# Silu at the ends of convolution blocks, k and q weighting behind the substitution, three casts on VectorE, in a two-layer hybrid encoder

## The chip, the cores and the metric

The kernel runs on one core of a Trainium2 chip. A core has the engines PE (TensorE), DVE (VectorE), ACT (ScalarE), POOL (GpSimd) and SP (SyncE, which only issues transfers here), each working through its own instructions in order, and 16 DMA engines that serve all queues. The metric is the device time of one execution in microseconds (us). For each kernel several executions are timed and the median counts.

## The reference, cut to what matters

Two layers over 256 rows of width 1024, fp32 throughout. Each layer has one wide input projection, a gated delta branch (8 heads of 128, a short convolution over q, k and v), a differential attention branch (8 heads), and a gated merge with an output projection.

```python
qkv = jax.nn.silu(short_conv(jnp.concatenate([q, k, v], axis=-1), conv_w))
q, k, v = jnp.split(qkv, (GDN_QK, 2 * GDN_QK), axis=-1)
q = l2norm(heads(q, GDN_DK)); k = l2norm(heads(k, GDN_DK)); v = heads(v, GDN_DV)
g = -jnp.exp(a_log) * jax.nn.softplus(ab[2:] + dt_bias)
...
L = jnp.where(strict, jnp.einsum('bhncd,bhnmd->bhncm', kb, k) * decay, 0.0)
T = lax.linalg.triangular_solve(eye + L, eye, lower=True, unit_diagonal=True)
...
qk = jnp.where(lower, jnp.einsum('bhncd,bhnmd->bhncm', q, k) * decay, 0.0)
S_t = a_t (I - b_t k_t k_t^T) S_(t-1) + b_t k_t v_t^T;  o_t = S_t^T q_t   (both directions)
y_a = rmsnorm(o) * silu(z_a);   y_b = attention(q_b, k_b, v_b) * silu(z_b)
x = x + (sigmoid(gate_a) * (y_a @ w_pa) + sigmoid(gate_b) * (y_b @ w_pb)) @ w_out
```

## The kernel before

**Projections.** A weight block of 1024 x 512 is loaded in four parts (kp 0 to 3, 512 KB each, by SP's queue) into three buffers called raw. Each part is split in two fp32r halves: ACT casts raw to hi (L230), DVE subtracts to get lo (L232). PE multiplies the activations hT with hi, again with the other half, and with lo (L244 to L246 row-major, accumulators pp_; L298 to L302 feature-major, accumulators pf_). hi and lo have two buffers each, so a part is cast when PE has finished with the part two before it. Projections are named by what they make: k, q, v of the delta branch (two blocks g of four each), qk (four: q and k of the attention branch), vb, zb, za, gb, pb, ga, pa, o.

**Convolution.** conv() runs a feature-major projection and closes each of its four 128-channel blocks: ACT writes the middle tap (cvq and the like, L523), four DVE instructions add the other taps (L527), ACT takes tanh of half the sum (thq, L531), and DVE multiplies (th + 1) * conv (L536), which is twice the Silu; the factor is taken out in the norms. Eight blocks each of k, q and v make 24 a layer. The result lies in kq; PE turns it (ctk, ctq, L544) and ACT sums its squares (sqj).

**Decays.** log_decays() takes the logarithms of gates and norms on ACT (Ln, L572), turns them into running sums with PE (grps) and copies those to grow on DVE (L588). POOL writes them to DRAM (gdr, L591) and decays() reads each of four groups back, spread to all partitions (B, 512 KB each, L618). POOL masks them (L624) and ACT takes 8 exps of 128x128 a group (L628). weigh_k() takes the grams of k (kk, PE, L611) and multiplies them with the summed decays into A (L635). weigh_q() multiplies the grams of q and k (kq) into B (L639).

**Substitution.** A goes through DRAM (adr) to la and lt; 31 steps on DVE (L670, L671) solve the triangular systems in X. spread_blocks() copies X to lt (L674), POOL writes both to DRAM (udr, L678), and blocks T and U are read back. merges() and chunks() then run the chunked recurrence on PE (zt, qs, ks and the like), with ktm, the turned k, weighted by POOL (L795). The attention heads (sc, mx, es: scores, maximum, exps; L839 to L848) and the zb and za projections run beside the substitution.

**What sets the order.** The program is written in the order of its calls, and a scheduler places each engine's instructions by priority; the loads and splits of weights run under high priority, ahead of their place. tc.issue_after(ins) keeps an instruction behind another one (held in the dictionary mark). SP's and POOL's queues take their transfers in that order too, and an instruction that waits holds up all behind it on its engine.

## Time and profile before

| | us |
|---|---|
| median of 3 runs | 779.93 |
| lowest, highest | 778.48, 781.05 |
| span of the profiled execution | 777.1 |
| PE busy | 758.2 |
| DVE busy | 557.3 |
| ACT busy | 474.9 |
| POOL busy | 101.9 |

The profiled execution has no time of its own beside its span; the runs lie 1.4 to 4.0 above that span. Busy time says how long an engine worked; with several engines, only the waits of the one that sets the end are worth something. The granted clock of PE is 1.00 in all windows but the last.

### The profile page before, as it was taken

How to read it: one execution, taken by the hardware profiler on the slowest of the kernel's cores; microseconds unless marked ns; L12 is line 12 of the kernel's file. 1: busy time of each engine (PE TensorE's matmuls, PEld its weight loads, DVE VectorE, ACT ScalarE, POOL GpSimd, SP SyncE). 2: the span in 40 equal slices, each digit the busy share in tenths (PEclk: the TensorE clock that was granted, in tenths of full speed). 3: DMA queues.
4: the chain of work that ended last, by engine and by line, in shares of the span. 5: the costliest groups of instructions: out<-in, count | busy, mean ns of one | idle time of the engine just before them, and what ended most of it. 6: DMA issues, size and time to landing. Idle time of an engine off the chain costs nothing.

```text
span 777.1 us, 13805 instructions
## 1 busy us (share of the span) xinstructions
PE 758.2 (98%) x5222; PEld 647.7 (83%) x5222; DVE 557.3 (72%) x1051; ACT 474.9 (61%) x1042; POOL 101.9 (13%) x137
## 2 busy tenths in 40 slices
PE   8999999999999999999999999999999999999996
PEld 4899879887778888887889888899777788888784
DVE  5686878999974635377677776989999553536782
ACT  5657776557677744564554668655577776356551
POOL 5100461100030100010010025510001110001000
PEclk9999999999999999999999999999999999999998
DMA  7752756554496644346664256755446954343631
GB/s 227 240 177 78 224 146 198 174 172 136 112 207 187 210 135 129 117 144 210 215 224 136 82 160 221 194 170 161 141 137 174 233 164 160 114 133 111 213 110 54
DMA packets 77745, 126.91 MB, mean 163 GB/s; under 512 B 19679, under 2 KB 20015, under 8 KB 77680
## 3 DMA queue, kind: packets, MB, share of 16 engines
q1 hardware_dynamic: 71038, 112.99, 48.4%
q0 software_dynamic: 3936, 9.77, 4.8%
q10 hardware_dynamic: 2706, 3.28, 1.3%
q8 instruction: 41, 0.67, 0.4%
q14 instruction: 24, 0.20, 0.1%
HBM read 121.27 MB, written 4.75 MB: 162 GB/s over the span
## 4 chain that ended last, share of the span: by engine, by line
PE 81%; DVE 7%; DMA 5%; ACT 4%; issue 2%; POOL 0%; SPq 0%; POOLq 0%; ACTq 0%; DVEq 0%
PE pp_vb L282 5%; DMA raw_q<-in_w_in_dram 3%; PE pp_qk L245 2%; PE pp_qk L246 2%; PE pp_qk L244 2%; PE pp_o L282 2%; PE pf_k L298 2%; PE pf_k L302 2%; PE pf_v L298 2%; PE pf_k L300 2%; PE pp_gb L245 2%; PE sc L839 2%; PE pp_gb L244 2%; PE pf_v L302 2%; PE pf_v L300 2%; PE av L865 2%
## 5 line engine op out<-in xcount | busy, mean ns | idle before, releaser
L245 PE MATMUL pp_qk<-lo_qk,hT 128*128 128x512 f32 x128 | 51.3, 401 | 1.0 <-DVE lo_qk L232 1.0
L246 PE MATMUL pp_qk<-hi_qk,hT 128*128 128x512 f32 x128 | 50.1, 391 | 0.0
L230 ACT CAST hi_qk<-raw_qk 128x1024 fp32r<-128x1024 f32 x32 | 33.5, 1046 | 23.6 <-PE pp_qk L246 12.6
L244 PE MATMUL pp_qk<-hi_qk,hT 128*128 128x512 f32 x128 | 46.1, 398 | 0.7 <-ACT hi_qk L230 0.7
L232 DVE TENSOR_TENSOR lo_qk<-raw_qk,hi_qk 128x1024 fp32r<-128x1024 f32 x32 | 40.2, 1257 | 7.6 <-ACT hi_qk L230 7.4
L232 DVE TENSOR_TENSOR lo_pb<-raw_pb,hi_pb 128x1024 fp32r<-128x1024 f32 x16 | 19.6, 1224 | 35.7 <-ACT hi_pb L230 35.7
L298 PE MATMUL pf_q<-hT,hi_q 128*128 128x256 f32 x128 | 36.5, 288 | 0.3 <-ACT hi_q L230 0.2
L298 PE MATMUL pf_v<-hT,hi_v 128*128 128x256 f32 x128 | 36.5, 289 | 0.0
L300 PE MATMUL pf_v<-hT,hi_v 128*128 128x256 f32 x128 | 36.2, 286 | 0.0
L300 PE MATMUL pf_q<-hT,hi_q 128*128 128x256 f32 x128 | 35.9, 284 | 0.0
L848 ACT ACTIVATE es<-sc,mx 128x256 f32<-128x256 f32 x64 | 29.8, 473 | 10.1 <-DVE mx L846 10.0
L298 PE MATMUL pf_k<-hT,hi_k 128*128 128x256 f32 x128 | 35.8, 285 | 0.0
L302 PE MATMUL pf_q<-hT,lo_q 128*128 128x256 f32 x128 | 35.7, 292 | 0.0
L300 PE MATMUL pf_k<-hT,hi_k 128*128 128x256 f32 x128 | 35.7, 283 | 0.0
L232 DVE TENSOR_TENSOR lo_gb<-raw_gb,hi_gb 128x1024 fp32r<-128x1024 f32 x16 | 19.6, 1224 | 22.2 <-ACT hi_gb L230 22.0
L232 DVE TENSOR_TENSOR lo_ga<-raw_ga,hi_ga 128x1024 fp32r<-128x1024 f32 x16 | 19.6, 1226 | 21.0 <-ACT hi_ga L230 21.0
L302 PE MATMUL pf_v<-hT,lo_v 128*128 128x256 f32 x128 | 34.6, 286 | 0.0
L302 PE MATMUL pf_k<-hT,lo_k 128*128 128x256 f32 x128 | 34.4, 285 | 0.0
L230 ACT CAST hi_pb<-raw_pb 128x1024 fp32r<-128x1024 f32 x16 | 16.8, 1049 | 25.1 <-PE pp_pb L246 24.3
L527 DVE SCALAR_TENSOR_TENSOR cvq<-pf_q,cw,cvq 128x254 f32<-128x254 f32 (+1 forms) x64 | 29.7, 476 | 1.8 <-ACT cvq L523 1.4
L527 DVE SCALAR_TENSOR_TENSOR cvv<-pf_v,cw,cvv 128x254 f32<-128x254 f32 (+1 forms) x64 | 30.2, 483 | 0.6 <-ACT cvv L523 0.5
L527 DVE SCALAR_TENSOR_TENSOR cvk<-pf_k,cw,cvk 128x254 f32<-128x254 f32 (+1 forms) x64 | 28.5, 478 | 2.0 <-ACT cvk L523 1.3
(356 smaller groups left out, 2495.5 us busy)
## 6 DMA issues: line engine op xcount, KB each, us to landing
raw_qk<-in_w_in_dram SPq DMA_DIRECT2D x32, 512.0 KB, 3.7
raw_k<-in_w_in_dram SPq DMA_DIRECT2D x16, 512.0 KB, 4.6
raw_q<-in_w_in_dram SPq DMA_DIRECT2D x16, 512.0 KB, 3.7
raw_v<-in_w_in_dram SPq DMA_DIRECT2D x16, 512.0 KB, 3.8
raw_zb<-in_w_in_dram SPq DMA_DIRECT2D x16, 512.0 KB, 3.6
raw_za<-in_w_in_dram SPq DMA_DIRECT2D x16, 512.0 KB, 3.7
raw_gb<-in_w_in_dram SPq DMA_DIRECT2D x16, 512.0 KB, 4.7
raw_o<-in_w_out_dram SPq DMA_DIRECT2D x16, 512.0 KB, 4.5
```

The lines of the kernel that those rows point to most:

```text
L230: high = S.copy(hi[:, :, :n], raw[:, :, :n]).ins
L232: mark[nm, kp] = high, V.tensor_tensor(lo[:, :, :n], raw[:, :, :n], hi[:, :, :n].bitcast(F32), ALU.subtract).ins
L244: T.matmul(o, act[kt // 4][:, 0, kt % 4, ts_], hi, start=kt == 0, stop=False)
L245: T.matmul(o, act[kt // 4][:, 0, kt % 4, ts_], lo, start=False, stop=False)
L246: mark["proj"] = T.matmul(o, act[kt // 4][:, 1, kt % 4, ts_], hi, start=False, stop=kt == KT - 1).ins
L282: mark["proj"] = T.matmul(o, a_, w_, start=kt == 0 and a_ is ah and w_ is hi, stop=kt == KT - 1 and a_ is al).ins
L298: T.matmul(o, hi[:, cs], act[kt // 4][:, 0, kt % 4, :], start=first, stop=False, skip_group_check=True)
L300: T.matmul(o, hi[:, cs], act[kt // 4][:, 1, kt % 4, :], start=False, stop=False, skip_group_check=True)
L302: T.matmul(o, lo[:, cs], act[kt // 4][:, 0, kt % 4, :], start=False, stop=done, skip_group_check=True)
L527: V.scalar_tensor_tensor(ca[:, o0:o1], acc[:, b, o0 + sft : o1 + sft], cw[:, j, cb : cb + 1], ca[:, o0:o1], ALU.mult, ALU.add)
L839: mm = T.matmul(sp[n][:, qt * SEQ : (qt + 1) * SEQ], qkT[h // 4][rows, 0, h % 4, qt * P : (qt + 1) * P], qkT[h // 4][rows, 1, h % 4, :], s ...
L848: S.activation(es[:, n, qt, :], spv[:, qt, :], AF.Exp, bias=mx[:, n, qt : qt + 1], accum_out=s_all[:, h, n, qt : qt + 1])
```

## The change

- **Silu.** In 18 of 24 convolution blocks a layer ACT writes Silu of the sum straight into kq (or into the buffer vf for v). The six blocks in HALF (the first four of q and the last two of v) keep tanh and the product, with taps scaled by 0.5 once a layer. Since the result is no longer doubled, the constants in the norms change.
- **Weighting.** weigh_q() moves from beside the q convolutions to behind the fifth head, and its kq grams are held behind marks of the merges. The k weighting stays in its call order, and ktm's product on POOL is held behind a udr write.
- **Casts.** Three weight parts a layer (the last of q's second block, the first two of the second qk block) are cast by DVE (turned).
- **Broadcasts.** The third and fourth decays() pass the last exps of the first group to issue_after for their transfer.

```diff
--- before.py
+++ after.py
@@ -26,6 +26,7 @@
 EPS = 1e-6
+HALF = (0, 1, 2, 3, 22, 23)
 HP = None
@@ -204,7 +205,7 @@
-    def weights(w, c0, n, nm, homes=(None,) * 4, ahead=True, later=None, spare=(), held=None):
+    def weights(w, c0, n, nm, homes=(None,) * 4, ahead=True, later=None, spare=(), held=None, turned=()):
@@ -227,17 +228,17 @@
                 with behind(act):
-                    high = S.copy(hi[:, :, :n], raw[:, :, :n]).ins
+                    high = (V.tensor_copy if kp in turned else S.copy)(hi[:, :, :n], raw[:, :, :n]).ins
                 with behind(dve):
...
-    def proj_tm(act, w, c0, n, evac, nm, places=(None,) * 4, spare=(), later=None):
+    def proj_tm(act, w, c0, n, evac, nm, places=(None,) * 4, spare=(), later=None, turned=()):
         accs = banks2(f"pp_{nm}")
-        for kt, hi, lo in weights(w, c0, n, nm, places, later=later, spare=spare):
+        for kt, hi, lo in weights(w, c0, n, nm, places, later=later, spare=spare, turned=turned):
             for m in range(NM):
@@ -284,11 +285,11 @@
-    def proj_fm(act, w, c0, evac, nm):
+    def proj_fm(act, w, c0, evac, nm, turned=()):
...
         accs = [a.rearrange("p (b t) -> p b t", b=2) for a in banks2(f"pf_{nm}")]
-        for kt, hi, lo in weights(w, c0, 512, nm, later=mark.pop("later", None)):
+        for kt, hi, lo in weights(w, c0, 512, nm, later=mark.pop("later", None), turned=turned):
             for b in range(4):
@@ -415,6 +416,8 @@
         V.tensor_copy(cw.rearrange("p t b -> p (t b)"), cw_ps[:, : TAPS * 24])
+        for b0, b1 in ((0, 4), (22, 24)):
+            V.tensor_scalar(cw[:, :, b0:b1], cw[:, :, b0:b1], 0.5, None, ALU.mult)
         prm = small.tile([P, 2, 16], F32, tag="prm", name=f"prm{l}")
@@ -455,7 +458,8 @@
                           pt.rearrange("p (b t) -> p b t", b=4), (DH ** -0.5, 1.0)[s_])
-                proj_tm(hT, wl, (C_QB, C_KB)[s_] + 512 * i, 512, evac_qk, f"qk{l}{s_}{i}")
+                proj_tm(hT, wl, (C_QB, C_KB)[s_] + 512 * i, 512, evac_qk, f"qk{l}{s_}{i}",
+                        turned=(0, 1) if (s_, i) == (0, 1) else ())
@@ -524,18 +528,19 @@
                         o0, o1 = max(0, -sft), SEQ - max(0, sft)
-                        V.scalar_tensor_tensor(ca[:, o0:o1], acc[:, b, o0 + sft : o1 + sft],
-                                               cw[:, j, cb : cb + 1], ca[:, o0:o1],
-                                               ALU.mult, ALU.add)
-                    th = work.tile([P, SEQ], F32, tag="vf", name=f"th{seg}{l}{g}{j4}", bufs=2)
-                    S.activation(th, ca, AF.Tanh, scale=0.5)
-                    if slot is None:
-                        f_ = th.rearrange("p (m t) -> p m t", m=NM)
+                        mark["conv"] = V.scalar_tensor_tensor(
+                            ca[:, o0:o1], acc[:, b, o0 + sft : o1 + sft],
+                            cw[:, j, cb : cb + 1], ca[:, o0:o1], ALU.mult, ALU.add).ins
+                    cm = ca.rearrange("p (m t) -> p m t", m=NM)
+                    if slot is None or cb in HALF:
+                        th = work.tile([P, SEQ], F32, tag="vf", name=f"th{seg}{l}{g}{j4}", bufs=2)
+                        tm = th.rearrange("p (m t) -> p m t", m=NM)
+                    f_ = tm if slot is None else kq[:, 4 * g + j4, :, slot, :]
+                    if cb in HALF:
+                        S.activation(tm, cm, AF.Tanh)
+                        V.scalar_tensor_tensor(f_, tm, 1.0, cm, ALU.add, ALU.mult)
                     else:
-                        f_ = kq[:, 4 * g + j4, :, slot, :]
-                    mark["conv"] = V.scalar_tensor_tensor(
-                        f_, th.rearrange("p (m t) -> p m t", m=NM), 1.0,
-                        ca.rearrange("p (m t) -> p m t", m=NM), ALU.add, ALU.mult).ins
+                        S.activation(f_, cm, AF.Silu)
                     vf.append(f_)
@@ -555,7 +560,8 @@
                                      accum_out=ss[:, m, hd : hd + 1])
-            proj_fm(hT, wl, c_base + 512 * g, evac_conv, f"{seg}{l}{g}")
+            proj_fm(hT, wl, c_base + 512 * g, evac_conv, f"{seg}{l}{g}",
+                    turned=(3,) if (seg, g) == ("q", 1) else ())
@@ -564,9 +570,9 @@
             kss = e_[:, :, 32:40]
-            V.tensor_scalar(kss, ssk, 4.0 * EPS, None, ALU.add)
+            V.tensor_scalar(kss, ssk, EPS, None, ALU.add)
             kh = small.tile([P, NM, NH], F32, tag="kh", name=f"kh{l}")
-            V.tensor_scalar(kh, kss, 1.0 / 16.0, None, ALU.mult)
+            V.tensor_scalar(kh, ssk, EPS, None, ALU.add)
             G.tensor_tensor(nrm.rearrange("p m h -> p (m h)"), kh.rearrange("p m h -> p (m h)"),
@@ -604,19 +610,21 @@
-        def gram(nm, g, c, slot):
+        def gram(nm, g, c, slot, after=None):
             gp = bank_c(f"{nm}{l}{g}{c}")
...
                 kqh = kq[:, 4 * g + j4, c]
-                T.matmul(gp[:, j4 * P : (j4 + 1) * P], kqh[:, 0, :], kqh[:, slot, :],
-                         start=True, stop=True)
+                with behind(after):
+                    T.matmul(gp[:, j4 * P : (j4 + 1) * P], kqh[:, 0, :], kqh[:, slot, :],
+                             start=True, stop=True)
             return heads4(gp)
-        def decays(g, c):
+        def decays(g, c, after=None):
             hs4 = slice(4 * g, 4 * g + 4)
             dec = B[:, c, hs4].rearrange("p h d i -> p d h i")
-            G.dma_start(out=B[:, c, hs4].rearrange("p h d i -> p (h d i)"),
-                        in_=gdr[c, hs4].rearrange("h d i -> (h d i)").partition_broadcast(P))
+            with behind(after):
+                G.dma_start(out=B[:, c, hs4].rearrange("p h d i -> p (h d i)"),
+                            in_=gdr[c, hs4].rearrange("h d i -> (h d i)").partition_broadcast(P))
             end = (P - 1) * (1 - c)
@@ -625,8 +633,8 @@
                     h = 4 * g + j4
-                    S.activation(dec[:, d, j4, :], dec[:, d, j4, :], AF.Exp,
-                                 bias=lnc[:, d, c, h : h + 1])
+                    mark["decay", d] = S.activation(dec[:, d, j4, :], dec[:, d, j4, :], AF.Exp,
+                                                    bias=lnc[:, d, c, h : h + 1]).ins
@@ -634,9 +642,9 @@
-        def weigh_q(g, c):
+        def weigh_q(g, c, after):
             bv = B[:, c, 4 * g : 4 * g + 4]
-            V.tensor_tensor(bv, gram("kq", g, c, 1).unsqueeze(2).to_broadcast([P, 4, 2, P]), bv, ALU.mult)
+            V.tensor_tensor(bv, gram("kq", g, c, 1, after).unsqueeze(2).to_broadcast([P, 4, 2, P]), bv, ALU.mult)
@@ -671,12 +679,12 @@
         def spread_blocks():
-            V.tensor_copy(lt, X.rearrange("p c i -> p i c"))
+            mark["spread"] = V.tensor_copy(lt, X.rearrange("p c i -> p i c")).ins
             for d in range(2):
...
                 for w, src_ in enumerate((X, lt) if d == 0 else (lt, X)):
-                    G.dma_start(out=udr[w, :, :, 8 * d : 8 * d + 8].rearrange("b g t j i -> (b g) (t j i)"),
-                                in_=src_[ps_].rearrange("p j i -> p (j i)"))
+                    mark["udr"] = G.dma_start(out=udr[w, :, :, 8 * d : 8 * d + 8].rearrange("b g t j i -> (b g) (t j i)"),
+                                in_=src_[ps_].rearrange("p j i -> p (j i)")).ins
@@ -792,7 +800,8 @@
             for d in range(2):
-                G.tensor_tensor(st[d], st[d], last(kds[:, d, hs4], P), ALU.mult)
+                with behind(mark["udr"]):
+                    G.tensor_tensor(st[d], st[d], last(kds[:, d, hs4], P), ALU.mult)
                 ps = four(f"sp{d}", lambda j: st[d][:, j, :], lambda j: y1[d][:, j, :])
@@ -896,20 +905,17 @@
         weigh_k(0, 0)
+        seen = mark["decay", 0], mark["decay", 1]
         decays(0, 1)
         weigh_k(0, 1)
-        decays(1, 0)
+        decays(1, 0, seen[0])
         weigh_k(1, 0)
-        decays(1, 1)
+        decays(1, 1, seen[1])
         weigh_k(1, 1)
         turn_blocks()
-        weigh_q(0, 0)
-        weigh_q(0, 1)
         conv("q", C_QA, 1, 1)
...
         qk_part(0, 1)
-        weigh_q(1, 0)
-        weigh_q(1, 1)
         substitute(0, 31)
@@ -928,6 +934,9 @@
         head(5)
+        for g in range(2):
+            for c in range(NM):
+                weigh_q(g, c, mark["done", 4 * g + 2 * c + 1])
         z_part(za, C_ZA, "za", 1)
@@ -982,7 +991,7 @@
         rq = small.tile([P, NM, NH], F32, tag="rq", name=f"rq{l}")
-        V.tensor_scalar(rq2, ssq, 0.25 * P, EPS * P, ALU.mult, ALU.add)
+        V.tensor_scalar(rq2, ssq, float(P), EPS * P, ALU.mult, ALU.add)
         G.tensor_tensor(rq.rearrange("p c h -> p (c h)"), rq2.rearrange("p c h -> p (c h)"),
```

Where instructions stand now. First ACT around the second q convolution block in layer 0: hi_q are weight casts of that block (its first one stands three rows ahead of this piece), stg copies of the first qk projection, B the exps of the decays, thq and cvq the first q block. Before:

```order
L443 COPY stg_1059<-pp_qk_985 128x512
L230 CAST hi_q_1234<-raw_q_1236 128x1024
L443 COPY stg_1072<-pp_qk_986 128x512
L531 ACTIVATE thq_964<-cvq_958 128x256
L523 ACTIVATE cvq_967<-pf_q_810,cw_268 128x256
L556 ACTIVATE sqj_280,ssq_333<-ctq_949 128x128 x2
L230 CAST hi_q_1264<-raw_q_1266 128x1024
L556 ACTIVATE sqj_280,ssq_333<-ctq_949 128x128
L456 ACTIVATE qkT_0_281<-qkt_1066 128x4x128
L556 ACTIVATE sqj_280,ssq_333<-ctq_949 128x128
L628 ACTIVATE B_340<-B_340,lnc_336 128x128 x8
L230 CAST hi_q_1294<-raw_q_1296 128x1024
```

After (L numbers of the changed program), from the second row behind the first hi_q on:

```order
L540 ACTIVATE thq_932<-cvq_926 128x256
L636 ACTIVATE B_342<-B_342,lnc_338 128x128 x4
L446 COPY stg_1045<-pp_qk_971 128x512
L636 ACTIVATE B_342<-B_342,lnc_338 128x128 x4
L540 ACTIVATE thq_950<-cvq_944 128x256
L231 CAST hi_q_1208<-raw_q_1210 128x1024
L446 COPY stg_1058<-pp_qk_972 128x512
L527 ACTIVATE cvq_953<-pf_q_796,cw_268 128x256
L636 ACTIVATE B_342<-B_342,lnc_338 128x128 x7
L561 ACTIVATE sqj_282,ssq_335<-ctq_935 128x128
L636 ACTIVATE B_342<-B_342,lnc_338 128x128
L231 CAST hi_q_1238<-raw_q_1240 128x1024
```

Eight exps now stand ahead of the block's second cast and eight more ahead of its third, where before the third stood ahead of all of them. 

DVE around grow in the same layer: lo_qk are the low halves of the first qk block, cvq taps of the first q block, ge, lnc, glog the gate logarithms. Before:

```order
L232 TENSOR_TENSOR lo_qk_1006<-raw_qk_1007,hi_qk_1005 128x1024
L573 SCALAR_TENSOR_TENSOR ge_315<-ga_312,ge_315 128x2x32
L527 SCALAR_TENSOR_TENSOR cvq_931<-pf_q_809,cw_268,cvq_931 128x254
L576 SCALAR_TENSOR_TENSOR lnc_336<-ge_315 128x16 x2
L579 TENSOR_TENSOR glog_788<-ge_315,nega_273 128x32
L232 TENSOR_TENSOR lo_qk_1024<-raw_qk_1025,hi_qk_1023 128x1024
L536 SCALAR_TENSOR_TENSOR kq_329<-thq_937,cvq_931 128x2x128
L527 SCALAR_TENSOR_TENSOR cvq_940<-pf_q_809,cw_268,cvq_940 128x254
L527 SCALAR_TENSOR_TENSOR cvq_940<-pf_q_809,cw_268,cvq_940 128x255
L588 COPY grow_795<-grps_790 8x512
L527 SCALAR_TENSOR_TENSOR cvq_940<-pf_q_809,cw_268,cvq_940 128x255
L232 TENSOR_TENSOR lo_qk_1042<-raw_qk_1043,hi_qk_1041 128x1024
```

After:

```order
L233 TENSOR_TENSOR lo_q_888<-raw_q_889,hi_q_887 128x1024
L579 SCALAR_TENSOR_TENSOR ge_317<-ga_314,ge_317 128x2x32
L582 SCALAR_TENSOR_TENSOR lnc_338<-ge_317 128x16 x2
L585 TENSOR_TENSOR glog_774<-ge_317,nega_275 128x32
L233 TENSOR_TENSOR lo_qk_974<-raw_qk_975,hi_qk_973 128x1024
L531 SCALAR_TENSOR_TENSOR cvq_917<-pf_q_795,cw_268,cvq_917 128x254
L531 SCALAR_TENSOR_TENSOR cvq_917<-pf_q_795,cw_268,cvq_917 128x255
L594 COPY grow_781<-grps_776 8x512
L531 SCALAR_TENSOR_TENSOR cvq_917<-pf_q_795,cw_268,cvq_917 128x255
L233 TENSOR_TENSOR lo_qk_992<-raw_qk_993,hi_qk_991 128x1024
```

The gate logarithms now stand ahead of the first lo_qk, and grow behind that and two taps of the first q sub-block.

POOL from the k weighting to the writes of the substitution's result. Before:

```order
L795 TENSOR_TENSOR ktm_330<-ktm_330,kds_341 128x512 x4
L654 DMA adr_342<-A_339 32x16x32 x4
L656 DMA la_344<-adr_342 64x1024
L657 DMA lt_345<-adr_342 64x1024
L658 MEMSET X_346 128x1024
L659 MEMSET X_346 128x32
L986 TENSOR_TENSOR rq_3662<-rq_3661,mhalf 128x16
L678 DMA udr_343<-X_346 8x8x1024 x2
L678 DMA udr_343<-lt_345 8x8x1024 x2
```

After:

```order
L662 DMA adr_344<-A_341 32x16x32 x4
L664 DMA la_346<-adr_344 64x1024
L665 DMA lt_347<-adr_344 64x1024
L666 MEMSET X_348 128x1024
L995 TENSOR_TENSOR rq_3634<-rq_3633,mhalf 128x16
L667 MEMSET X_348 128x32
L686 DMA udr_345<-X_348 8x8x1024 x2
L804 TENSOR_TENSOR ktm_332<-ktm_332,kds_343 128x512 x4
L686 DMA udr_345<-lt_347 8x8x1024 x2
```

The four ktm products moved from ahead of the adr writes to between the two pairs of udr writes. On SP's queue, the four loads of U now stand ahead of the last raw_za load; before, they stood behind it, one raw_gb load and four loads of T.

## The prediction

> **What bounds the kernel now.** I read the page's busy row and chain first, then the windows, then PE's waits.
>
> ```profile
> span 777.1 us, 13805 instructions
> PE 758.2 (98%) x5222; PEld 647.7 (83%) x5222; DVE 557.3 (72%) x1051; ACT 474.9 (61%) x1042; POOL 101.9 (13%) x137
> PE 81%; DVE 7%; DMA 5%; ACT 4%; issue 2%; POOL 0%; SPq 0%; POOLq 0%; ACTq 0%; DVEq 0%
> ```
>
> PE works in 98% of the span, and the change leaves PE's matmuls as they are. A faster kernel can only come from the 777.1 - 758.2 = 18.9 us in which PE stands. The windows (span, then PE busy and its instructions, then PEld, DVE, ACT, POOL) say where they lie:
>
> ```profile
> 0.00:20.00 20.00, 16.05 (x47) 9.50 (x47) 11.51 (x25) 11.93 (x20) 11.19 (x24) 1.00 0.79 225
> 100.00:120.00 20.00, 18.46 (x111) 15.80 (x111) 16.34 (x21) 15.28 (x43) 11.43 (x11) 1.00 0.52 147
> 470.00:490.00 20.00, 18.45 (x137) 16.82 (x136) 13.77 (x21) 17.72 (x55) 13.84 (x16) 1.00 0.59 200
> 610.00:640.00 30.00, 29.37 (x543) 23.98 (x543) 15.88 (x37) 22.14 (x59) 3.14 (x2) 1.00 0.62 192
> 740.00:777.00 37.00, 29.33 (x134) 24.04 (x132) 18.61 (x23) 12.36 (x19) 1.75 (x4) 0.92 0.22 81
> ```
>
> The first 20 us lose 3.95 and the last 37 lose 7.67; the edit touches neither. That leaves 18.9 - 3.95 - 7.67 = 7.3 us, **the most that can be won**. The stage around the k grams loses 1.54 in layer 0 and 1.55 in layer 1, 3.1 together, and 610 to 640 loses 0.63. Who ends PE's waits:
>
> ```profile
> PE kk L611 <- DVE A L635: 1.3, 2, 0.8
> PE pp_qk L245 <- DVE lo_qk L232: 1.0, 2, 0.5
> PE pp_zb L244 <- ACT es L848: 0.9, 2, 0.5
> PE pp_qk L244 <- ACT hi_qk L230: 0.7, 2, 0.5
> PE zt L737 <- issue: 0.6, 1, 0.6
> ```
>
> The kk and pp_qk rows are the stage of 3.1 us: kk grams follow each other on PE there, and each waits for the A product that reads its bank.
>
> **The change, part by part.** The sum is made against the profiled execution, span 777.1; the median of the runs, 779.93, lies 2.8 above it, and I carry that over.
>
> *Work taken from DVE and ACT.* The rows, busy and then the mean in ns:
>
> ```profile
> L536 DVE SCALAR_TENSOR_TENSOR kq<-thq,cvq 128x256 f32<-128x256 f32 x16 | 6.7, 432 | 1.5 <-ACT thq L531 1.5
> L639 DVE TENSOR_TENSOR B<-kq,B 128x1024 f32<-128x1024 f32 x8 | 9.8, 1221 | 0.4 <-PE kq L611 0.4
> L795 POOL TENSOR_TENSOR ktm<-ktm,kds 128x512 f32<-128x512 f32 x8 | 12.9, 1640 | 8.2 <-ACT kds L651 8.2
> ```
>
> 18 closing products a layer go: 36 x 0.43 = 15.5 us off DVE. Three weight casts a layer come to DVE; the nearest row, the 128x1024 copy to lt quoted below, takes 1.12, so 6 x 1.12 = 6.7 us come. The four q weightings a layer (4 x 1.22 = 4.9 us) move behind the substitution. None of this is on PE's path by itself: DVE is busy 72% and PE 98%. It shortens what runs ahead of the substitution's end by 4.9 us and ten closing products, 4.3 us, so 9 us at most; the places of the lo_za casts in DVE's order allow only some 6. This is what makes U and the zt products early, so I book the 0.6 of zt as won.
>
> *Table loads.* They go from 7 to 13. The row that shows one, and its follower:
>
> ```profile
> 76.81 1.28 ACT L572 ACT_TABLE_LOAD   x1
> 78.10 0.27 ACT L572 ACTIVATE ge<-ge 128x80 f32<-128x80 f32 x1
> ```
>
> 6 x 1.28 = 7.7 us come to ACT and six casts of 1.05 leave it. ACT is busy 61%, so only a load with PE behind it can cost: the one ahead of the first es of each layer, where PE already waits for es (0.9). Bounds: -0.9 if DVE's relief makes es early, +2 x 1.28 - 0.9 = +1.7 if all of the load shows but what ACT idles there. I take 0. The Trainium skill, "ScalarE: Activation LUTs", section "What ACT_TABLE_LOAD costs", puts a switch of set at about 2.66 us with a drain of 1.38. Here the Ln starts 1.29 after the load began: this trace shows no such drain. By the page the six would be 16 us, and the es row would cost up to 2 x 2.66 - 0.9 = 4.4.
>
> *Log decays earlier.* In the new order Ln stands ahead of hi_qk's casts, so the gate logs leave earlier, and DVE's copy to grow stands behind the first lo_qk and two taps instead of some ten rows later.
>
> ```profile
> 76.15 0.48 DVE L527 SCALAR_TENSOR_TENSOR cvq<-pf_q,cw,cvq 128x255 f32<-128x255 f32 x1
> 82.69 0.67 DVE L588 COPY grow<-grps 8x512 f32<-8x512 f32 x1
> 86.71 2.18 POOL L618 DMA_DIRECT2D B<-gdr  x4 [1.84 <-ACT E L597]
> 93.19 1.15 POOL L621 TENSOR_TENSOR kds<-B,lnc 128x4 f32<-128x4 f32 x1 [4.30 <-DMA B<-gdr]
> 94.96 2.45 ACT L628 ACTIVATE B<-B,lnc 128x128 f32<-128x128 f32 x8 [0.93 <-POOL B L624]
> ```
>
> The second tap ends at 76.6, so grow starts there, 6.1 before 82.69. The rest follows at the same distances: broadcasts issued at 80.6, the first landed at 87.1, first exps at 88.9. The four broadcasts stand together in POOL's order as before: the edges meant to hold two of them back tie a POOL transfer to ACT's exps, and the order shows no effect of them.
>
> *What ACT does until then.* This carries the forecast.
>
> ```profile
> 85.22 1.05 ACT L230 CAST hi_q<-raw_q 128x1024 fp32r<-128x1024 f32 x1 [2.17 <-PE pp_qk L246]
> 86.18 0.41 ACT L531 ACTIVATE thq<-cvq 128x256 f32<-128x256 f32 x1
> 88.75 1.05 ACT L230 CAST hi_q<-raw_q 128x1024 fp32r<-128x1024 f32 x1
> 91.59 0.28 PE L298 MATMUL pf_q<-hT,hi_q 128*128 128x256 f32 x1
> 95.47 0.36 PE L298 MATMUL pf_q<-hT,hi_q 128*128 128x256 f32 x1
> ```
>
> Before, the second hi_q cast runs at 88.75 and the exps come after all but the last hi_q. Now eight exps stand right behind the first hi_q, ahead of two stg copies and the second hi_q, and eight more ahead of the third. ACT is free at 86.6 and waits until 88.9 for the broadcast. Eight exps (2.45), a stg copy (about 0.5) and a tanh (about 0.3) follow: the second hi_q runs from 92.15 to 93.2, its lo on DVE ends at 94.4. PE wants that pair from 91.59 on (some 92.0 with the transposes that now stand ahead), its lo half four matmuls later, at 92.5. So PE loses 94.4 - 92.5 = 1.9. The third pair comes 4.7 later by the same addition (lo at 99.1) and is wanted at 97.7: another 1.4. **3.3 us a layer, 6.6 in all.** Bounds: 0, if the broadcast comes when ACT gets there; above, the broadcast at its old time (exps at 94.96, 6.1 later than I reckon), which adds 6.1 to 1.9, 8.0 a layer. I take 3.3 since the grow row that moves stands close behind rows whose times are known.
>
> The broadcasts also meet other loads. Issues with size and us to landing (middle number of the last field), and the software queue in 90 to 92:
>
> ```profile
> B<-gdr POOLq DMA_DIRECT2D x4, 512.0 KB, 8.8
> raw_q<-in_w_in_dram SPq DMA_DIRECT2D x1, 512.0 KB, 10.7
> q0 software_dynamic: 112, 0.42, 100.8%
> 80.93 0.37 SPq L226 DMA_DIRECT2D raw_q<-in_w_in_dram  x1
> ```
>
> The raw_q load issued 1.2 us behind the first broadcast took 10.7 us. Now the second raw_q (80.93) stands there: landed at 91.6, just before ACT gets to its cast at 92.15, so nothing is added. The Trainium skill, "DMA: Bandwidth & Descriptors", section "Queues, rings and completion order", has each DMA engine take turns between its queues; the row with 100.8% for one queue, while that load waited, disagrees. By the page raw_q would land some us sooner, which also changes nothing here.
>
> *The k grams.* They move into the next projection, twelve matmuls apart on two banks; A's product has time between them. I book the whole 3.1 as won.
>
> *POOL and SP behind the substitution.* The ktm products (4 x 1.64 = 6.6) now stand between the two pairs of udr writes; U's four loads stand ahead of the last raw_za on SP.
>
> ```profile
> 216.15 1.12 DVE L674 COPY lt<-X 128x1024 f32<-128x1024 f32 x1
> 216.71 1.25 POOL L678 DMA_DIRECT2D udr<-X  x2 [72.29 <-DVE X L671]
> 225.15 1.96 SPq L705 DMA_DIRECT2D T<-udr  x4
> udr<-lt POOLq DMA_DIRECT2D x2, 256.0 KB, 6.5
> raw_za<-in_w_in_dram SPq DMA_DIRECT2D x2, 512.0 KB, 5.2
> 232.39 0.39 PE L244 MATMUL pp_za<-hi_za,hT 128*128 128x512 f32 x1
> ```
>
> With X ready 6 to 9 us earlier (lt from 207 to 210), udr of lt is issued 1.1 + 1.25 + 6.6 later, lands after 6.5, U's four issues take 2 (as T's four do), raw_za lands 5.2 later and its cast takes 1.05: 230.7 to 233.7, wanted at 232.39 plus PE's net delay of 1.75. I take 0 here.
>
> **Sum:** -3.1 (grams) + 6.6 (hi_q behind the exps) - 0.6 (zt) + 0 (es) + 0 (raw_za) = +2.9: 780.0 for the span, **782.8** on the median.
>
> **Rivals.**
> *ACT never waits (faster).* If the first broadcast lands by 84.8, the exps fill idle time and hi_q is no later than PE wants it: 779.9 - 3.1 - 0.6 = 776.2; with all 7.3 won, 772.6. For it: ACT's 39% of idle time, and that the fourth hi_q, late for its load, cost PE only 0.2 (the window's row and PE's wait):
>
> ```profile
> 98.61 1.05 ACT L230 CAST hi_q<-raw_q 128x1024 fp32r<-128x1024 f32 x1 [1.20 <-DMA raw_q<-in_w_in_dram]
> PE pf_q L298 <- ACT hi_q L230: 0.2, 1, 0.2
> ```
>
> Against it: the broadcast lands 6.5 behind its issue however idle ACT is, and it is issued behind grow.
> *The waits trade evenly.* The new wait is 1.6 to 2.2 a layer and just replaces the grams': about 780.
> *raw_za behind U (slower).* If X gains less than 7 us, each us missing shows in za1: 2 us a layer more, 786.8. For it: ktm's 6.6 in the way; against: SP's queue had that load landed long before.
> *The broadcast is as late as before (slower).* 8.0 a layer: 779.9 + 16 - 3.7 = 792.2. For it: the exps' place in ACT's order, which lets nothing pass; against: the grow row.
> *The page's price of a table load* at es: 782.8 + 4.4 = 787.2; the 76.81 row speaks against it.
>
> **How the numbers follow.** A measurement tells a change from none from about 0.3%, 2.3 us: faster is below 777.6, slower above 782.2. Forecast 0.40 (spread of 2.5 us about 782.8: 0.24 slower, 0.16 within), ACT never waits 0.28 (0.27 faster, 0.01 within), even trade 0.05 (within), raw_za 0.15, late broadcast 0.07, table loads 0.05 (all slower). Faster 0.27, same 0.22, slower 0.51. The range is 774 to 789; the forecast's own is 780 to 785.5.
>
> **What would show it.** Right: PE's waits lose the kk and pp_qk rows and gain pf_q waiting for hi_q and lo_q of the last q projection, some 3 us in each layer; ACT idles about 2 us ahead of the first exps, ended by POOL or the broadcast; grow near 77. Wrong: a broadcast that lands by 85, no pf_q wait, or a new wait of pp_za for hi_za near 233, or of PE for es above 1 us a layer.

## The result, and the profile after

The changed kernel takes 791.42 us (median; 790.5 to 794.28), the one before, run beside it, 779.2 (778.08 to 781.05). The ratio is 1.0163, with a 95% interval of 1.0147 to 1.0178: slower by 12.2 us, where 2.9 were forecast, and outside the forecast range. The profiled execution took 791.06; its span is 788.7, 11.6 more than before.

The page's head for the changed kernel: span, then busy time of each engine, then the chain of waits by engine.

```profile
span 788.7 us, 13794 instructions
PE 763.9 (97%) x5222; PEld 651.4 (83%) x5222; DVE 559.1 (71%) x1025; ACT 481.3 (61%) x1042; POOL 93.7 (12%) x137
PE 80%; DMA 7%; DVE 7%; ACT 3%; issue 2%; POOL 0%; SPq 0%; POOLq 0%; ACTq 0%; DVEq 0%
```

PE still has its 5222 matmuls, but is busy for 763.9, not 758.2. So the 11.6 fall into two halves: PE stands 24.8 instead of 18.9 (+5.9), and **works 5.7 longer on the same instructions**. The first half is in PE's waits (us in total, times, longest):

```profile
PE pf_q L303 <- DVE lo_q L233: 3.4, 4, 1.4
PE pf_q L299 <- ACT hi_q L231: 1.9, 2, 1.4
PE at L868 <- DVE es L865: 1.8, 3, 1.4
PE pp_qk L246 <- DVE lo_qk L233: 1.4, 1, 1.4
PE ctq L549 <- DVE kq L541: 1.2, 2, 0.8
PE pf_k L303 <- DVE lo_k L233: 0.6, 2, 0.3
```

The kk row, the hi_qk row and the zt row of before are gone. In their place stand pf_q's two rows, 5.3 together (2.0 in layer 0, 3.4 in layer 1), and at's row, 1.8.

The second half has two parts that the trace names. Windows in the last q projection of layer 0 (us, then PE busy, PEld, DVE, ACT, POOL, the granted clock, DMA share, GB/s):

```profile
91.00:98.10 7.10, 5.21 (x38) 4.25 (x36) 4.50 (x9) 5.55 (x15) 5.20 (x11) 1.00 0.81 315
98.10:101.50 3.40, 3.29 (x15) 3.29 (x16) 3.07 (x10) 3.40 (x11) 0.00 (x0) 0.50 0.55 157
101.50:106.00 4.50, 3.61 (x31) 3.41 (x30) 3.79 (x5) 4.50 (x17) 0.00 (x0) 1.00 0.17 27
```

PE stands 1.9 there, and behind it comes a stretch of 3.4 us at clock 0.50, in which half the work is done: 1.7 lost that no row of waits holds. The other part is the group of the attention scores (busy, mean ns of one), before and then after:

```profile
L839 PE MATMUL sc<-qkT 64*128 64x256 f32 x128 | 20.8, 405 | 0.0
L848 PE MATMUL sc<-qkT 64*128 64x256 f32 x128 | 23.4, 410 | 0.0
```

One matmul takes as long as before, but together they cover 2.6 us more: 128 of 0.41 us would be 52 one after the other, so these 64-row matmuls overlap each other, and fewer do so in the new order. If all of it adds to PE's busy time, 1.7 + 2.6 is 4.3 of the 5.7; the rest isn't assigned to a group.

### The profile page after: what moved, and what is told of

Same layout as the page of the kernel before. It is cut to its first block, busy times and chain, and to the rows that moved or that the text cites. A ratio compares the mean times of both kernels' runs of the same rounds, so it can differ in the third digit from the quotient of the medians.

```text
span 788.7 us, 13794 instructions
## 1 busy us (share of the span) xinstructions
PE 763.9 (97%) x5222; PEld 651.4 (83%) x5222; DVE 559.1 (71%) x1025; ACT 481.3 (61%) x1042; POOL 93.7 (12%) x137
## 4 chain that ended last, share of the span: by engine, by line
PE 80%; DMA 7%; DVE 7%; ACT 3%; issue 2%; POOL 0%; SPq 0%; POOLq 0%; ACTq 0%; DVEq 0%
PE pp_vb L283 5%; PE pp_qk L246 3%; DMA raw_q<-in_w_in_dram 3%; PE pp_qk L247 3%; PE pp_qk L245 3%; PE pp_o L283 2%; DMA raw_vb<-in_w_in_dram 2%; PE pp_gb L246 2%; PE pp_gb L247 2%; PE pp_gb L245 2%; PE pp_pb L247 2%; PE pp_pb L246 2%; PE pp_pb L245 2%; PE pp_ga L247 2%; PE pp_ga L245 2%
## 5 line engine op out<-in xcount | busy, mean ns | idle before, releaser
L231 ACT CAST hi_qk<-raw_qk 128x1024 fp32r<-128x1024 f32 x28 | 29.4, 1048 | 30.5 <-PE pp_qk L247 19.6
L246 PEld LDWEIGHTS pp_qk<-lo_qk,hT 128*128 128x128 f32 x128 | 24.0, 188 | 7.6 <-DVE lo_qk L233 2.7
```

The lines of the kernel that those rows point to most:

```text
L231: high = (V.tensor_copy if kp in turned else S.copy)(hi[:, :, :n], raw[:, :, :n]).ins
L246: T.matmul(o, act[kt // 4][:, 0, kt % 4, ts_], lo, start=False, stop=False)
```

## The experiments

Medians in us; the kernel before stood beside each at 778.9 to 780.3. "Clock" is the median granted clock over the runs of a kernel: the one before has 0.997 to 0.998, the changed one 0.993, which on 790 us is some 3 us of lost work more. "pf_q" adds PE's waits there for hi_q and lo_q. All waits are read from one profiled execution of each kernel; those of e3 (786.0) and e10 (796.0) took longer than their medians, those of e14 (779.2) and e18 (787.9) less.

| run | kernel | median | ratio, interval | clock | pf_q |
|---|---|---|---|---|---|
| e1 | changed, exps later | 790.73 | 1.0152 (1.0110-1.0193) | 0.994 | 5.4 |
| e2 | changed, q weighting and ktm back | 788.09 | 1.0118 (1.0103-1.0133) | 0.995 | 4.8 |
| e3 | changed, no Silu | 781.88 | 1.0034 (1.0011-1.0056) | 0.996 | 1.4 |
| e4 | before, Silu alone | 795.28 | 1.0217 (1.0198-1.0236) | 0.994 | 5.1 |
| e5 | changed, broadcasts held | 796.39 | 1.0220 (1.0201-1.0239) | 0.994 | 0 |
| e6 | before, casts alone | 781.47 | 1.0028 (1.0014-1.0042) | 0.995 | 2.9 |
| e7 | held, q weighting and ktm back | 787.77 | 1.0109 (1.0086-1.0132) | 0.996 | 0 |
| e8 | changed, ktm back | 787.64 | 1.0106 (1.0091-1.0121) | 0.994 | 5.1 |
| e9 | before, ktm moved alone | 786.75 | 1.0101 (1.0088-1.0114) | 0.993 | 1.1 |
| e10 | held, ktm back | 790.77 | 1.0166 (1.0139-1.0193) | 0.996 | 0 |
| e11 | no Silu, ktm back | 784.45 | 1.0067 (1.0055-1.0080) | 0.996 | 1.6 |
| e12 | held, ktm on DVE | 787.86 | 1.0113 (1.0099-1.0128) | 0.998 | 0 |
| e13 | changed, no Silu in k | 794.27 | 1.0194 (1.0177-1.0211) | 0.988 | 1.8 |
| e14 | no Silu, ktm on DVE | 780.95 | 1.0017 (1.0007-1.0027) | 0.996 | 1.0 |
| e15 | before, ktm on DVE alone | 782.02 | 1.0037 (1.0025-1.0049) | 0.998 | 0 |
| e16 | no Silu in k, ktm on DVE | 784.86 | 1.0072 (1.0058-1.0087) | 0.997 | 1.8 |
| e17 | changed, ktm on DVE | 791.59 | 1.0142 (1.0116-1.0169) | 0.994 | 4.2 |
| e18 | Silu in k only, ktm on DVE | 790.12 | 1.0124 (1.0100-1.0149) | 0.994 | 5.8 |

### Which part costs: e2, e3, e4, e6

**e2** puts the q weighting and ktm back in their old places; **e3** closes all 24 blocks with tanh and the product again; **e4** is the kernel before with Silu in 18 blocks; **e6** is the kernel before with the three casts on DVE.

```diff
e2
-                with behind(mark["udr"]):
+                with behind(None):
...
+        weigh_q(0, 0, None)
+        weigh_q(0, 1, None)
e3
-HALF = (0, 1, 2, 3, 22, 23)
+HALF = tuple(range(24))
e4 (of before)
+                        S.activation(f_, cm, AF.Silu)
e6 (of before)
+                    high = (V.tensor_copy if kp in turned else S.copy)(hi[:, :, :n], raw[:, :, :n]).ins
```

> The changed kernel with the k and q weighting of q and ktm's product put back to their old places; Silu, casts and edges stay. Theory 1: at most 1 us from 791.4, since the exps keep their place. Theory 2: the scores of the heads, in 24 groups on PE in the changed kernel and 18 before, come together again (22 groups by the order), and 2 to 4 us go, to 787 to 789.5. Theory 3: 791.

> The changed kernel with tanh and the product in all 24 blocks (taps halved for all of them); moved weighting, the three casts on DVE and the edges stay. 7 table loads instead of 13, and the exps stand behind the third hi_q again. Theory 1: 782 to 785 (the kk waits of 3 us come back, the 5.3 us for hi_q and lo_q go). Theory 2: 791 to 794, since the weighting stays where it is and DVE gets its products back. Theory 3: as theory 1 but with the 1.7 us of the k projections gone as well, 780 to 782.

> The kernel before with Silu at the ends of 18 blocks as the only edit (HALF, taps, norms); no moved weighting, no casts on DVE, no edges. 13 table loads, exps ahead of the second hi_q as in the changed kernel. Theory 1: the waits for hi_q and lo_q are there, 786 to 790. Theory 2: 779 to 781. Theory 3: 785 to 790, with waits of PE for the casts and products that follow a table load rather than for hi_q and lo_q of the last q projection.

> The kernel before with the three weight casts a layer on DVE as the only edit that moves work; tanh in all 24 blocks with halved taps, weighting and broadcasts as before. Theory A: ACT gets free earlier in the stage of the exps; without Silu the broadcast is as late as before the change, so the kk waits (3.1 us) shrink: 776 to 779. Rival: the casts cost DVE what ACT gains, 779 to 782.

e2 won 3.3, e3 9.5. Silu alone costs 16.2, the casts alone 2.6. With Silu in, adding the casts (and the edges of the broadcasts) wins (e4 to e2: -7.2): the parts don't add up. That they work through the order, and that the casts relieve ACT where Silu's order loads it, is the likely reason; no run changes the order alone.

e2 and e6 came out in a range that was named (theory 2, the rival), e3 just below theory 1's and in theory 3's, e4 above all three. Theory 2's reason for e2, scores that come together, isn't the main one: e8, below, wins as much with the scores at 23.5.

### The exps ahead of hi_q: e1, e5, e7

The forecast had the second and third hi_q cast late for the exps ahead of them on ACT. **e1** holds the exps back on ACT; **e5** leaves them and holds the four broadcasts with a POOL instruction that reads a late kq block; **e7** is both, with q weighting and ktm back.

```diff
e1
+                    with behind(mark["qkT", 0]):
+                        mark["decay", d] = S.activation(dec[:, d, j4, :], dec[:, d, j4, :], AF.Exp, ...
e5
+        late = G.tensor_tensor(hold, kq[:, 1, 0, 1, :4], kq[:, 1, 0, 1, 4:8], ALU.add).ins
-        decays(0, 0)
+        decays(0, 0, late)
...
```

> The changed kernel with one edit: every exp of the decays is held on ACT behind the first turned copy of the first qk block (qkT), so that in ACT's order all casts of the second q block but the last stand ahead of the exps again, as before the change. Nothing is left out. Theory 1 (the exps at the head of ACT's line make hi_q and lo_q late): PE's waits for hi_q and lo_q in the last q projection, 5.3 us in the changed kernel, go, and with them the stretch of half clock; 791.4 falls by 5 to 9, to 782 to 786. Theory 2 (the moved k and q weighting costs PE the time around the heads): 790 to 792, the waits elsewhere unchanged. Theory 3 (table loads on ACT): no change either, 790 to 792.

> The changed kernel with the four broadcasts of the decays held on POOL behind a small POOL addition that reads the second closed block of the first q convolution, so that they are issued about where they were before the change against the loads (some 1.5 us behind the first cast of the second q block). By the order ACT then has its exps behind the third hi_q again. Nothing is left out. Theory A (after the run with the exps moved alone: two covers of one stall, the exps in ACT's line and the raw_q load that runs beside the broadcasts; both come from the early broadcast): PE's waits for hi_q and lo_q in the last q projection fall from 5.3 us to under 1.5, the kk waits of up to 3 us come back in part; 791.4 falls by 4 to 8, to 783.5 to 787.5. Rival B (hi_q is late for DVE and ACT work of the Silu blocks, not for the broadcast): the waits stay, 789 to 792. Rival C (a broadcast 7 us later makes the exps, A and the substitution late): the waits move to kk or zt, 790 to 794.

> The changed kernel with the broadcasts held as in the run before and the k and q weighting put back to its old place: Silu and casts stay. Theory A: the two gains add, -4 to -8 for the broadcast and -3.3 for the weighting (788.1 against 791.4): 780 to 784. Rival B: 786 to 789, no better than the weighting put back alone. Rival D (Silu costs in every stage through its table loads): over 785 with waits of PE for casts and closing blocks in the k, qk and zb stages.

e1 didn't remove the wait. ACT's timeline (start, length, what it waited for) in the changed kernel, then in e1:

```profile
91.21 1.28 ACT L636 ACTIVATE B<-B,lnc 128x128 f32<-128x128 f32 x4 [1.68 <-POOL B L632]
95.79 1.04 ACT L231 CAST hi_q<-raw_q 128x1024 fp32r<-128x1024 f32 x1 [1.34 <-DMA raw_q<-in_w_in_dram]
```

```profile
94.92 1.05 ACT L231 CAST hi_q<-raw_q 128x1024 fp32r<-128x1024 f32 x1 [4.39 <-DMA raw_q<-in_w_in_dram]
```

With the exps gone, the second hi_q waits 4.39 for its own load, and starts only 0.9 earlier. The load runs beside the early broadcasts. In the changed kernel it is issued at 84.47, and the issues between 83 and 86 us (size, us to landing) are

```profile
84.47 0.37 SPq L227 DMA_DIRECT2D raw_q<-in_w_in_dram  x1
raw_q<-in_w_in_dram SPq DMA_DIRECT2D x1, 512.0 KB, 11.2
B<-gdr POOLq DMA_DIRECT2D x4, 512.0 KB, 8.7
```

So the wait had two covers of nearly one length, exps and load. e5 takes both away, and the hi_q and lo_q rows are gone as expected; yet the kernel is 5 us slower, since PE meets another wait (next part). In e7, with ktm out of the way, pf_q's rows are gone too (in e2 they are 4.8), and 0.3 is won, less than the runs can tell: PE then waits for DVE. Of the expectations, e1 came out where theories 2 and 3 had it, e5 above all three ranges, e7 where rivals B and D had it; its waits, for casts and closing blocks, are of D's kind.

```profile
PE pp_qk L246 <- DVE lo_qk L233: 2.5, 2, 1.2
PE ctq L549 <- DVE kq L541: 2.5, 2, 1.2
PE pp_qk L245 <- DVE hi_qk L231: 1.6, 2, 0.8
```

### ktm on POOL: e8, e9, e10, e12, e15

**e8** takes only ktm back, **e9** makes only that move in the kernel before, **e10** is e5 with ktm back, **e12** is e5 with ktm computed by DVE, **e15** the kernel before with ktm on DVE.

```diff
e8, e10
-                with behind(mark["udr"]):
+                with behind(None):
e9 (of before)
+                with behind(mark["udr"]):
+                    G.tensor_tensor(st[d], st[d], last(kds[:, d, hs4], P), ALU.mult)
e12, e15
-                    G.tensor_tensor(st[d], st[d], last(kds[:, d, hs4], P), ALU.mult)
+                V.tensor_tensor(st[d], st[d], last(kds[:, d, hs4], P), ALU.mult)
```

> The changed kernel with the four ktm products of POOL alone put back ahead of the adr writes; Silu, moved q weighting, casts and edges stay. Theory K (POOL's four products in a row hold up a DVE instruction that reads SBUF for the whole 4 us: es in the changed kernel, lo_za in the runs e3 and e5): DVE's longest es product falls from 4.9 us to 0.5, and 2 to 4 us go, 787.5 to 789.5, as with the whole weighting put back (788.1). Rival (the q weighting's place costs, not ktm's): 790.5 to 792.

> The kernel before with the four ktm products on POOL held behind the udr writes as the only edit. Theory K: one DVE instruction a layer takes 4 to 6 us beside them, near 217 and 595; whether PE feels it depends on which one: 779 if it is none that PE waits for soon, up to 788 if lo_za. Rival (the length of that instruction has another cause): no DVE instruction over 2 us there, 778 to 780.

> The changed kernel with the broadcasts held (as in e5) and ktm put back to its old place; Silu, moved q weighting and casts stay. Theory A with K: the waits for hi_q and lo_q of the last q projection stay gone and the waits of 4.3 us a layer for lo_za go too, with the half clock behind them: 796.4 - 8.5 - 3.4 = 784.5, between 782 and 787. Rival: lo_za is late for the order of the q weighting on DVE, 794 to 797.

> The changed kernel with the broadcasts held (as in e5) and the four ktm products a layer computed by DVE instead of POOL, in the same place of the program; nothing is left out. Theory K: no DVE instruction near 205 and 591 takes over 2 us, the waits for lo_za of 4.3 us a layer and the half clock behind them go: 796.4 - 8.5 - 3.4 + at most 2 x 2.8 of added DVE work = 784.5 to 788. Rival (DVE's own order makes lo_za late): 794 to 798.

> The kernel before with the ktm products on DVE as the only edit. Theory K: lo_qk and dsum beside them lose their extra 0.5 and 0.3 us a layer, DVE gains 2.8 us of work a layer at a place where it has time: 776.5 to 779.5. Rival (POOL's products cost nothing there and DVE is short of time): 779.5 to 783.

Timeline of the changed kernel, DVE and POOL:

```profile
213.00 5.26 DVE L865 SCALAR_TENSOR_TENSOR es<-es,cc 128x256 f32<-128x256 f32 x2
213.54 4.03 POOL L804 TENSOR_TENSOR ktm<-ktm,kds 128x512 f32<-128x512 f32 x4
223.39 0.88 DVE L865 SCALAR_TENSOR_TENSOR es<-es,cc 128x256 f32<-128x256 f32 x2
```

Two es products take 0.88 alone and 5.26 beside ktm: the second stands until all four POOL instructions are through. e9 shows the same 5.26 with nothing else changed, and is 7.8 us slower than before. There PE feels it: it stands 2.6 us in the ten from 220 and 2.8 in the ten from 600, each with 1.6 to 1.7 lost to half clock behind it. Its waits are these; two of the three for es stand there, the third, of 1.1, near 248:

```profile
PE at L860 <- DVE es L857: 3.9, 3, 1.5
PE pp_za L244 <- DVE za L313: 2.6, 2, 1.3
```

In the changed kernel PE hardly feels it: of the 1.8 in the row of at, PE's turning of es, only 0.2 a layer stands beside the products, and 1.4 is one wait at 251, which is also in e8 and e17, where no ktm product is near. In e5 the DVE instruction is a lo_za cast, which PE waits for in each layer:

```profile
205.08 5.90 DVE L233 TENSOR_TENSOR lo_za<-raw_za,hi_za 128x1024 fp32r<-128x1024 f32 x1
205.86 4.03 POOL L804 TENSOR_TENSOR ktm<-ktm,kds 128x512 f32<-128x512 f32 x4
211.03 0.50 PE L246 MATMUL pp_za<-lo_za,hT 128*128 128x512 f32 x1 [4.27 <-DVE lo_za L233]
```

```profile
207.90:211.30 3.40, 0.27 (x1) 0.27 (x2) 3.40 (x2) 0.00 (x0) 3.40 (x6) 1.00 0.19 56
211.40:214.80 3.40, 3.40 (x14) 3.02 (x13) 2.35 (x7) 2.04 (x8) 1.11 (x3) 0.50 0.83 218
```

The windows are of e5: PE nearly idle, then the same 3.4 us at half clock. e12 has no ktm on POOL, no such wait, clock 0.998, and wins 8.5 against e5. e8 wins 3.8, all that e2 won, so of the moved weighting it is ktm's place that costs. How the 3.8 comes about in the changed kernel is shown only in part: in the profile of e8 PE stands 2.0 less, 0.4 of it where es had stood beside ktm, but 1.4 at a lo_qk near 139, where DVE's copy to la no longer waits for its transfer. ktm's product isn't free on DVE either (e15: +2.8); in the changed kernel DVE's price takes back what POOL's place costs (e17, 791.6, wins nothing by the medians and 1.6 by the ratios). In e10 PE waits 3.6 for a lo_v, but not beside ktm: DVE stands at the copy to la, 20 us behind the products, which waits 4.9 for its transfer.

e8, e9 and e12 came out in theory K's ranges, e15 in its rival's, e10 between its two.

### Silu by its blocks: e11, e13, e14, e16, e17, e18

All are the changed kernel; **e11** has no Silu and ktm back, **e13** no Silu in the eight k blocks. The four others have ktm on DVE: **e14** no Silu, **e16** Silu in q and v alone, **e18** in k alone, **e17** in all 18.

```diff
e11, e14
+HALF = tuple(range(24))
e13, e16
+HALF = (0, 1, 2, 3, 8, 9, 10, 11, 12, 13, 14, 15, 22, 23)
e18
+HALF = tuple(range(8)) + tuple(range(16, 24))
```

> The changed kernel without Silu (tanh in all 24 blocks, halved taps) and with ktm in its old place; what is left of the change is the q weighting behind the fifth head and the three casts on DVE. Theory K: the waits for lo_za of 2.1 us a layer and the half clock go from the 781.9 of e3: 774 to 778, faster than before the change. Rival: the q weighting's place or the casts cost as much as they save, 779 to 782.

> The changed kernel with tanh and the product kept in the eight k blocks as well (Silu in 10 of 24 blocks); all else as changed. By the order the exps stand behind the third hi_q again and the k stage has no table load. Theory A: the waits for hi_q and lo_q go and the k stage is as before; theory K adds that ktm on POOL then meets lo_za as in e3: about 782, as e3 (781.9) with Silu in q and v costing little, 780 to 785. Rival (Silu costs everywhere): 787 to 791.

> The changed kernel without Silu and with the ktm products on DVE: what is left is the q weighting behind the fifth head and the three casts on DVE. Theory K: neither the 2.1 us a layer for lo_za of e3 nor the 1.8 us a layer for lo_qk of e11 is there, and no half clock: 773 to 777, faster than before the change. Rival: 780 to 784, as e3 and e11.

> The changed kernel with tanh kept in the k blocks too (Silu in 10 of 24) and the ktm products on DVE; nothing is left out. Theory K: the lo_za instruction of 5.9 us of e13 and the waits of 4.3 us behind it go, with two stretches of half clock a layer: 794.3 - 8.6 - 3.4 to 6.8 = 779 to 782.5. If Silu in q and v costs nothing, it comes out as e14 (781.0); if Silu costs wherever it stands, 784 to 788.

> The changed kernel with one edit: ktm's product on DVE. Theory: ktm on POOL behind the udr write costs 3.8 (as its old place showed) and Silu the rest, with or without the broadcast held, so 787 to 789 (787.9 was measured with the broadcast held), the es row gone or below 1 and the hi_q and lo_q rows of about 5 us together still there. Rival: the broadcast beside the projection costs nothing by itself and holding it costs 2 or more; then 784 to 786.

> The changed kernel with ktm on DVE and Silu in the eight k blocks only; the q and v blocks close by tanh and the product. No Silu gave 781.0, Silu in q and v alone 784.9. If the cost goes by the block, 8 k blocks beside 10 give 781.0 + 8/10 x 3.9 = 784.1, range 783.3 to 785, and the scores stay at 23.4 busy. If the scores' place on PE (21.2 without Silu, 23.4 with it in q and v) is most of the cost and comes with any Silu: 783 with the scores at 23.4. If Silu in k costs nothing by itself: 780 to 782 with the scores near 21.

The four on DVE make a square. Since the kernel before ran at 780.3 beside e17 and e18 and at 779.1 and 779.2 beside e16 and e14, I take them by their ratios to it, times 779.2: none +1.3, q and v +5.6, k +9.7, all +11.1. Silu in the **k** blocks costs 8.4 by itself and 5.5 beside the others; in q and v 4.3 and 1.4. By the intervals of the table each figure is good to 1 to 3 us. The e18 expectation fell on all three of its readings: none had k dearer than q and v. e14 and e16 came out in their rivals' ranges, e11, e13 and e17 above all of theirs.

One reason for k is in the order. DVE's, POOL's and ACT's rows of e14, then of e18:

```profile
83.02 0.67 DVE L594 COPY grow<-grps 8x512 f32<-8x512 f32 x1
87.04 2.19 POOL L626 DMA_DIRECT2D B<-gdr  x4 [1.83 <-ACT E L603]
89.08 1.05 ACT L231 CAST hi_q<-raw_q 128x1024 fp32r<-128x1024 f32 x1
94.24 3.62 ACT L636 ACTIVATE B<-B,lnc 128x128 f32<-128x128 f32 x12
```

```profile
78.26 0.68 DVE L594 COPY grow<-grps 8x512 f32<-8x512 f32 x1
82.28 2.19 POOL L626 DMA_DIRECT2D B<-gdr  x4 [1.82 <-PE gcps L600]
88.97 1.28 ACT L636 ACTIVATE B<-B,lnc 128x128 f32<-128x128 f32 x4
94.90 1.05 ACT L231 CAST hi_q<-raw_q 128x1024 fp32r<-128x1024 f32 x1 [2.69 <-DMA raw_q<-in_w_in_dram]
```

Without Silu in k the log decays, the broadcasts and the exps stand where they stood before the change; with it they stand 4.8 us earlier, the exps ahead of the second hi_q. All seven kernels with Silu in k and unheld broadcasts (the changed one, e1, e2, e4, e8, e17, e18) have pf_q waits of 4.2 to 5.8; the others have at most 1.8, but for e6 (2.9, of which 1.7 is for the hi_q that DVE casts).

Holding the broadcasts by hand (e17 to e12) wins 3.7 by the medians, 2.3 by the ratios, and brings the clock from 0.994 to 0.998, which is 0.004 x 790 = 3.2; in part the waits move on, in e12 to ctq, which waits 2.5 for DVE's kq. So the early broadcasts are a quarter to a third of the 9.8 that Silu costs here (e14 to e17): with them held, the 18 blocks still cost 7.5 (e14 to e12, by the ratios). What makes up these 7.5 isn't shown. The scores go with a part of it, 21.2 busy in e14, 23.4 in e12 and e16, 22.4 in e18. Less what the half clock adds, PE's busy time is 755.8 to 758.5 in the kernels whose scores take 20.8 to 21.3 and 758.3 to 764.0 in those with 23.4 to 23.8. The loads of ACT's tables go with Silu too, and no run takes them away alone.

e13 has no pf_q wait for hi_q either and is slow, with ktm on POOL: DVE's lo_za falls beside it as in e5 (wait 8.6, clock 0.988). e16, the same with ktm on DVE, is 9.4 faster. Without Silu, ktm behind udr gives 781.9 (e3) and at its old place 784.5 (e11): here the old place is the worse one, where DVE's lo_qk stands beside it (PE waits 3.6). **None of the 18 beats the kernel before**; e14, at 1.0017, comes nearest.

## Why the prediction was wrong

Its direction was right and its first term was about right, in part by luck; what it booked at nothing made the difference.

- *Exps ahead of hi_q, +6.6.* Right in place, and the size is near: pf_q waits of 5.3, with a stretch of half clock behind one; holding the broadcasts that bring it about wins 2.3 to 3.7 (e17 to e12). ACT waits 1.7 ahead of the first exps, ended by POOL, where about 2 were forecast. Grow starts at 78.95, not at 76.6; forecast was "near 77". "Nothing is added" by the raw_q load failed: the load was taken at its old issue, 80.93, but is issued at 84.47, when a raw buffer comes free behind DVE's lo_qk, takes 11.2 us, not 10.7, and holds the second hi_q by 1.34 beyond ACT's own line. That cast starts at 95.79 instead of 92.15, and PE gets there at 96.4 instead of 92.0. Both ends of the wait lie some 4 us later than reckoned, so the fit of its size is partly luck.
- *Grams, -3.1.* Right in kind: the kk and hi_qk rows, 2.0, are gone. But lo_qk's 1.0 came back as 1.4 at another place, where it stands behind DVE's copy to la, which waits 2.52 for its transfer:

```profile
136.66 1.13 DVE L672 COPY la<-lt 64x1024 f32<-64x1024 f32 x1 [2.52 <-DMA lt<-adr]
```

- *zt, -0.6.* Right: its row is gone.
- *ktm behind udr, 0.* **The first step that failed.** The prediction weighed ktm's 6.6 us only as a delay in POOL's queue, with raw_za and U behind it; that delay indeed cost nothing (no wait for hi_za). It didn't ask what DVE does meanwhile. The ktm row it quoted, 1.64 each, held a sign: where DVE stands the products take 1.04, which suggests that before POOL was slowed beside DVE. Now DVE is the one that stands, 4.4 us. The term measures 3.8 in this kernel (e8) and 7.8 alone (e9). That DVE's standing is the cause is shown in e9 and e5, where PE waits for it; in the changed kernel PE waits only 0.4 there, and the way of the other 3.4 stays open. The Trainium skill, "SBUF — State Buffer", section "SBUF: two separate sides", has a port pair that DVE and GpSimd share as an exclusive lock for a whole instruction, taken also by DVE operations with two SBUF inputs and given to the one that starts first. The 5.26 and the 5.90 agree with such a block; but the DVE instruction waits for four POOL instructions here, not for one, and by the trace of e5 it had started first.
- *"The change leaves PE's matmuls as they are."* **The second step that failed.** Their count stayed, their time did not: +5.7, of which the scores' new order can be 2.6 and the half clock behind waits is 1.7 in this execution and about 3 by the clock of all runs. The sum had no term for either, and took only PE's idle 18.9 as what could change.
- *Silu itself.* Beyond the exps ahead of hi_q the sum gave it no cost. It costs 9.5 in the changed kernel (e3), and 7.5 with the broadcasts held and ktm on DVE (e14 to e12). Which of its waits make up the larger part stays open.
- *es, 0 (-0.9 to +1.7).* The forecast wait, of pp_zb for es, is gone (0.4 for stg stands there). Another came, of at for es: 1.6 in layer 0, so that the sign "PE for es above 1 us a layer" was met. Its larger part, 1.4 at 251, has no cause that a run shows; it stays when ktm moves.
- *Table loads, 0.* One shows ahead of the closing of k: it starts only when its activation's data is there.

```profile
46.17 1.28 ACT L543 ACT_TABLE_LOAD   x1 [1.25 <-DVE cvk L531]
47.47 0.42 ACT L543 ACTIVATE kq<-cvk 128x256 f32<-128x256 f32 x1
```

It took 1.28 with nothing behind it, as the prediction read it; the 2.66 of the Trainium skill, "ScalarE: Activation LUTs", section "What ACT_TABLE_LOAD costs", doesn't show here either. PE's waits for what this ACT order makes late (ctq, lo_k) are 1.8 together, with no row before; that the loads cause them wasn't tried by itself.

- *Rivals.* The late broadcast gave 792.2, nearest to the result, by a mechanism that didn't occur: the broadcasts are 3.7 us earlier than before, and holding them wins where ktm is off POOL (e17 to e12). raw_za behind U didn't occur.

Out of the profile the sum would be: waits +6.1 (pf_q +5.1, at +1.8, ctq and lo_k +1.8, start +0.9, others -3.5), scores +2.6, half clock +1.7: 10.4 of the 11.6 of the profiled executions. Open is how the scheduler comes to other places for the scores and the decays by Silu in a block; the runs show that it does, not the rule. That fewer scores overlap as the cause of their 2.6 is read from busy and mean time; the order of the scores was not changed by itself.

## What to carry to other kernels

Where a scheduler sets the order, cheaper instructions early in the program are a change of everything behind them: take the new order first, and then ask of each engine what now stands beside what, not only behind what. A product moved to POOL's idle time is not free if DVE reads two operands at that time (e9: 7.8 us). With PE near 98% busy, a wait costs its length and, where PE stands for half of a piece of 3.41 us (last section), another 1.7 for the clock behind it; but taking a wait away may only bring up the next one (e2 to e7).
